# The output projection of a hybrid decoder layer: queueing the residual loads with their products, and a reversed order of token halves for the upper channels

## The chip, the cores and the metric

The kernel runs on one core of one Trainium2 chip. The metric is the device time of one execution in microseconds. In the trace PE is the matrix engine (its weight loads are listed as PEld), DVE the vector engine, ACT the scalar engine, POOL GpSimd, and SP the engine whose queue issues most of the loads.

## The reference

One layer of a hybrid decoder on 576 tokens (512 of a prompt and 64 of eight running sequences), width 1024. Two branches, an RWKV-7 scan and a differential attention, are merged by gates into `m`; then

```python
m = gate_a * (o_a @ lp['w_br_a']) + gate_b * (o_b @ lp['w_br_b'])
x = x + m @ lp['w_out']
hn = rmsnorm(x, lp['g_ffn'], NORM_EPS)
x = x + jnp.square(jax.nn.relu(hn @ lp['w_up'])) @ lp['w_down']
```

and a final RMSNorm. The change lies in the second of these lines and in how its result is made ready for `w_up`.

## The kernel before

Activations lie transposed, with channels on the 128 partitions and the 576 tokens along the free axis, so `x` is eight blocks of 128 channels (`d` = 0 to 7). Every fp32 product is made of three products of rounded halves: a tile is split into `hi` (ACT, a rounding copy) and `lo` (DVE, the rest), and PE adds hi·hi, hi·lo and lo·hi. The helper `dense` runs `stream`: the weights of one block of output channels are loaded by SP in two pieces of four 128x128 blocks (tiles `raw_...`, three buffers), each piece is split (`hi_...`, `lo_...`, three buffers each), and then the two halves of the tokens (`HALF`, 288 each) are computed one after the other, 24 matmuls each, into one of two PSUM banks (`ps_...`). When a half is done, `evac` is called for it.

The stage of the change is the loop of line 1085, over d = 0, 4, 1, 5, 2, 6, 3, 7. For each d it loads a block of x's rows (`xr`, two buffers, line 1087), and `evac` (here `ev`, line 1091) adds it to the product (`ya`, DVE), scales by g_ffn (`hf`, ACT) and puts the result, split in two, into blocks for the next stage. That stage, `up_pair`, multiplies by `w_up` by a scheme with seven products of quarter size in place of eight; so it wants not only the blocks b11 (channels 0 to 3, first half of tokens), b21 and b22 (channels 4 to 7, first and second half) but also the sums t1, t2, t3 and t4 of blocks. With lower block h of channel k and upper block h' of channel k + 4: t1 = second half of h minus first half of h; t2 = second half of h' minus t1; t3 = second half of h' minus second half of h; t4 = first half of h' minus t2. Each goes through `put`: an ACT copy and a DVE subtraction. `up_pair` uses them in the order t1, b11, t2, b21, t3, b22, t4. Behind each d, ACT squares the block and POOL adds it to `acc` for the norm.

The order on each engine's queue is made by a planner when the program is built: among the instructions whose predecessors and whose tile's place in memory are ready, it takes the one with the smallest priority number. By default that number is the place in the program, counted up from zero; `prio(at)` sets another. Loads of weights have `FEED + 1000 * job` with FEED = -1000000, where `job` counts the products in order, so every one of them is taken ahead of what has a default number. Evacuations have `FEED + 1000 * job + 200`. The loads of `w_up` (tiles `a`, line 1143) have the number of a job behind all eight of this stage. On the chip each queue keeps the order that it was given, and an instruction at its head that waits holds up all behind it. The load of `xr` has the default number. The places of `xr`, `hf` and `a` in memory were held before by tiles of the stage ahead of this one, the last of which are `g` (the gates that the branch product `ps_bra` is merged with), whose last reader is the DVE instruction that makes `ml`.

Of the kernel before, what the change touches and what calls it, by code (L numbers as in the profile page):

```python
# [8 lines left out]
F32 = mybir.dt.float32  # L9
# [6 lines left out]
P = 128  # L16
D = 1024
KT = D // P
# [10 lines left out]
HALF = ((0, 288), (288, 288))  # L29
# [12 lines left out]
def tile_hybrid_step(ctx, tc, xT, xsT, ktab, vtab, s0T, ptab, w_in, vecs, w2a2, g2, lamv,  # L42
                     w_bra, w_brb, w_out, w_up, w_down, cst, bias_p, bias_s,
                     yT, kTo, vTo, Sp, Ss, sh):
    nc = tc.nc
# [3 lines left out]
    def pool(name, bufs=1, stack=ctx, **kw):  # L49
        return stack.enter_context(tc.tile_pool(name=name, bufs=bufs, **kw))  # L50

    def f32(ap):
        return ap.bitcast(F32)

    ring = {"job": 0}

    def act(out, in_, func=AF.Copy, **kw):
        ring["act"] = AE.activation(out=out, in_=in_, func=func, **kw)  # L58

    def tt(out, a, b, op, eng=None):  # L60
        ins = (eng or VE).tensor_tensor(out=out, in0=a, in1=b, op=op)  # L61
        if eng is None:
            ring["tt"] = ins
# [19 lines left out]
    FEED, LATE, FILL = -1000000, 500000, 1000000  # L83

    @contextmanager
    def prio(at):
        was, tc.cur_priority = tc.cur_priority, at
        yield
        tc.cur_priority = was

    MUL, ADD, SUB, MAX = ALU.mult, ALU.add, ALU.subtract, ALU.max
# [42 lines left out]
    def v(i, n=1):  # L134
        return vec[:, i:i + n]
# [65 lines left out]
    def finish(gen, at=None):  # L201

        n = 0
        if at is None:
            at = next(gen, None)
        while at is not None:
            with prio(FILL + at + n):
                at = next(gen, None)
            n += 1

    def dense(*args, **kw):
        finish(stream(*args, **kw))
# [53 lines left out]
    with tc.tile_pool(name="xin", bufs=2, reuse_waits="tile") as xin:  # L266
# [6 lines left out]
        for k in range(0, KT, 4):  # L273
            for j in range(3):
                with prio(FEED + 1000 + 10 * k + j):
                    name = f"raw_{'qkv'[j]}0_{k}"
                    if k == 0:
                        raw = ring["pool"].tile([P, 4, P], F32, tag="raw", name=name, bufs=3)
                    else:
                        raw = zw.tile([P, 1 + NX], F32, tag="z" if j else "tz", name=name,  # L280
                                      bufs=2 if j else 1)[:, :4 * P].rearrange("p (k w) -> p k w", k=4)
# [152 lines left out]
    def gate(g):  # L434

        gg = gs.tile([P, NT], F32, tag="gg", name=f"gg{g}")

        def ev(ps, t0, n):
            tt(gg[:, t0:t0 + n], ps, R1[:, t0:t0 + n], MUL)
            act(gg[:, t0:t0 + n], gg[:, t0:t0 + n], AF.Tanh, scale=0.5)  # L440
        yield from stream(w_in[26 + g], KT, xh, xl, HALF, ev, f"g{g}")
        nc.sync.dma_start(out=gt_d[g], in_=gg)
# [20 lines left out]
    def branch_b(d):  # L463

        if not ob:
            ob.extend(ob_halves())
        gg = rt.tile([P, NT], F32, tag="T", name=f"gb{d}", bufs=6)
        nc.sync.dma_start(out=gg, in_=gt_d[KT + d])

        def ev(ps, t0, n):  # L470
            stt(gg[:, t0:t0 + n], gg[:, t0:t0 + n], 1.0, ps, ADD, MUL)
        yield from stream(w_brb[d], HB, ob[0], ob[1], HALF, ev, f"brb_{d}")
        nc.sync.dma_start(out=gt_d[KT + d], in_=gg)
# [160 lines left out]
    for h in range(HB):  # L634
        if h:
            qkv(h)
        for cc in range(2):
            GE.tensor_copy(
                out=qbd[64 * cc:64 * cc + 64, :, h, 8 * cc:8 * cc + 8],
                in_=qT[64 * cc:64 * cc + 64, h, NPR:].rearrange("p (b q) -> p b q", b=NB))  # L640
# [406 lines left out]
    mh = mp.tile([P, KT, NT], F32R, name="mh")  # L1047
    ml = mp.tile([P, KT, NT], F32R, name="ml")
    for d in range(KT):
        g = []  # L1050
        for i in range(2):
            gg = rt.tile([P, NT], F32, tag="T", name=f"g{i}_{d}", bufs=6)
            nc.sync.dma_start(out=gg, in_=gt_d[KT * i + d])
            g.append(gg)

        def ev(ps, t0, n, d=d, g=g):
            a, b = (x[:, t0:t0 + n] for x in g)
            stt(a, a, 1.0, ps, ADD, MUL)
            tt(a, a, b, ADD)
            act(mh[:, d, t0:t0 + n], a, scale=0.5)  # L1060
            stt(ml[:, d, t0:t0 + n], a, 0.5, f32(mh[:, d, t0:t0 + n]), MUL, SUB)
        dense(w_bra[d], HB, [o[:, 0] for o in oab], [o[:, 1] for o in oab], HALF, ev, f"bra_{d}")
# [15 lines left out]
    wt_ = pool("wt", 2, stack=fin, side="right", reuse_waits="tile")  # L1078

    def put(n, k, src):  # L1080
        act(hb[n][:, 0, k], src)
        tt(hb[n][:, 1, k], src, f32(hb[n][:, 0, k]), SUB)

    hfs = {}
    for i, d in enumerate((0, 4, 1, 5, 2, 6, 3, 7)):
        xr = wt_.tile([P, NT], F32, tag="xr", name=f"xr{d}")
        nc.sync.dma_start(out=xr, in_=xT[:, d])
        hf = hfs[d] = wt_.tile([P, NT], F32, tag="hf", name=f"hf{d}", bufs=3)
        k = d % 4

        def ev(ps, t0, n, d=d, k=k, xr=xr, hf=hf):
            x, h = ya[:, d, t0:t0 + n], hf[:, t0:t0 + n]
            tt(x, ps, xr[:, t0:t0 + n], ADD)
            act(h, x, scale=v(V_GF + d))
            if d < 4:
                if t0 == 0:
                    put("b11", k, h)
                else:
                    t1 = wt_.tile([P, 288], F32, tag="t", name=f"t1_{k}", bufs=4)
                    tt(t1, h, hf[:, :288], SUB)  # L1100
                    hfs["t1", k] = t1
                    put("t1", k, t1)
            elif t0 == 0:
                put("b21", k, h)
            else:
                t2 = wt_.tile([P, 288], F32, tag="t", name=f"t2_{k}", bufs=4)
                t3 = wt_.tile([P, 288], F32, tag="t", name=f"t3_{k}", bufs=4)
                t4 = wt_.tile([P, 288], F32, tag="t", name=f"t4_{k}", bufs=4)
                tt(t2, h, hfs["t1", k], SUB)
                put("t2", k, t2)  # L1110
                tt(t3, h, hfs[k][:, 288:], SUB)
                put("t3", k, t3)
                put("b22", k, h)
                tt(t4, hf[:, :288], t2, SUB)
                put("t4", k, t4)
        dense(w_out[d], KT, mh, ml, HALF, ev, f"wo{d}")
        sq = (M2, R2)[i % 2]
        act(sq, ya[:, d], AF.Square)
        if i == 0:
            GE.tensor_copy(out=acc, in_=sq)  # L1120
        else:
            tt(acc, acc, sq, ADD, GE)
# [137 lines left out]
    for d, n in enumerate((None, "t1", "b11", "t2", "b21", "t3", "b22", "t4")):  # L1260
        if n:
            t = fp.tile([P, 2, 4, 288], F32R, tag=f"h_{n}", name=f"w3_{d}", bufs=1)
            t = t.rearrange("p i k t -> p (i k t)")
# [179 lines left out]
```

## Time and profile before

| | |
|---|---|
| median of 3 runs | 1041.78 us (1041.49 to 1045.85) |
| the profiled execution, its own time | 1044.17 us |
| its span in the trace | 1042.4 us |
| PE busy | 1004.3 us, 96% of the span |
| the stage of the change | its first matmul starts at 578.7 us, its last at 639.6 us |

The profile is of one execution. A timeline row gives the start in us from the span's start, the busy time in us, the engine, the line, the operation with output and inputs, and in square brackets how long the engine was idle ahead of it and what it waited for. Rows that merge several instructions of a kind carry a count (x3). Matmuls overlap, so their pace is the distance from one start to the next, not the busy time of a row.

### The profile page before, as it was taken

Reading aid. Unit: us, or ns where it says so; the run is one execution under the profiler, and the core shown is the slowest. Engines: PE = TensorE matmul, PEld = TensorE weight load, DVE = VectorE, ACT = ScalarE, POOL = GpSimd, SP = SyncE. Lnnn points to the kernel's source line nnn. Section 1 sums busy time; section 2 is a strip of 40 time slices with the busy share of each in tenths; the row PEclk is TensorE's granted clock in tenths of the full one; section 3 lists DMA queues with packets and bytes.
Section 4 is the critical chain, followed back from the end, with each engine's and each line's share of the span. In section 5 each row is a group of like instructions: output and inputs, shape, how many; then the busy total and the mean of one; then the engine's idle time right before and its main releaser. Section 6 shows DMA issues by size and latency. Waiting matters only on the chain.

```text
span 1042.4 us, 24557 instructions
## 1 busy us (share of the span) xinstructions
PE 1004.3 (96%) x10088; PEld 931.2 (89%) x10088; DVE 690.2 (66%) x1445; ACT 498.5 (48%) x1090; POOL 94.9 (9%) x173
## 2 busy tenths in 40 slices
PE   9999989999999999999999799999999999999996
PEld 8989777888887879887889799999999999999996
DVE  6787545674856578435568788976666666666754
ACT  7575544443436344434334456655444444444732
POOL 1511100201010231000120021000000000000001
PEclk9999999999999989999999899999999999999998
DMA  7422444311112124322258542232222322221302
GB/s 273 170 81 76 135 147 139 94 45 51 36 53 65 45 94 146 98 67 89 90 172 253 187 123 86 82 102 82 91 89 86 100 91 82 91 82 41 112 21 91
DMA packets 50817, 105.75 MB, mean 101 GB/s; under 512 B 6050, under 2 KB 8098, under 8 KB 50578
## 3 DMA queue, kind: packets, MB, share of 16 engines
q1 hardware_dynamic: 47426, 96.95, 28.9%
q0 software_dynamic: 1648, 5.35, 1.4%
q8 instruction: 79, 1.29, 0.5%
q10 hardware_dynamic: 1632, 1.89, 0.5%
q14 instruction: 32, 0.26, 0.1%
HBM read 89.38 MB, written 14.78 MB: 100 GB/s over the span
## 4 chain that ended last, share of the span: by engine, by line
PE 77%; DVE 6%; ACT 5%; issue 5%; DMA 4%; POOL 2%; SPq 0%; DVEq 0%; POOLq 0%; ACTq 0%
PE ps_dn L72 20%; PE ps_g L72 10%; PE ps_z L72 7%; PE ua L1179 5%; PE ux L1179 5%; PE ps_bra L72 2%; PE uc L1179 2%; PE ps_k L72 2%; PE ud L1179 2%; PE ub L1179 2%; PE ps_q L72 2%; DMA kp<-in_ktab_dram 2%; PE pch L72 2%; PE pA L72 2%; PE pY L72 1%
## 5 line engine op out<-in xcount | busy, mean ns | idle before, releaser
L72 PE MATMUL ps_dn<-q,hi_dn 128*128 128x288 f32 x768 | 154.8, 296 | 0.0
L72 PEld LDWEIGHTS ps_dn<-q,hi_dn 128*128 128x128 f32 x768 | 122.8, 188 | 1.4
L72 PE MATMUL ps_dn<-q,lo_dn 128*128 128x288 f32 x384 | 113.2, 295 | 0.0
L72 PE MATMUL ps_g<-xh,lo_g 128*128 128x288 f32 x256 | 81.8, 319 | 0.1
L72 PE MATMUL ps_g<-xh,hi_g 128*128 128x288 f32 x256 | 81.1, 317 | 0.0
L72 PE MATMUL ps_g<-xl,hi_g 128*128 128x288 f32 x256 | 81.1, 317 | 0.0
L72 PEld LDWEIGHTS ps_dn<-q,lo_dn 128*128 128x128 f32 x384 | 72.0, 188 | 0.0
L72 PE MATMUL ps_z<-xh,hi_z 128*128 128x288 f32 (+1 forms) x224 | 69.1, 309 | 0.4 <-ACT hi_z L58 0.4
L72 PE MATMUL ps_z<-xh,lo_z 128*128 128x288 f32 (+1 forms) x224 | 69.5, 312 | 0.0
L72 PE MATMUL ps_z<-xl,hi_z 128*128 128x288 f32 (+1 forms) x224 | 68.7, 307 | 0.0
L61 DVE TENSOR_TENSOR ya<-ya,ps_dn 128x288 f32<-128x288 f32 x96 | 43.4, 452 | 29.4 <-PE ps_dn L72 29.3
L58 ACT ACTIVATE hi_dn<-raw_dn 128x512 fp32r<-128x512 f32 x48 | 30.1, 628 | 56.2 <-PE ps_dn L72 56.1
L1179 PE MATMUL ua<-h_b,hi 128*128 128x288 f32 x256 | 53.3, 298 | 0.4 <-ACT p L58 0.4
L72 PEld LDWEIGHTS ps_g<-xh,hi_g 128*128 128x128 f32 x256 | 50.2, 196 | 3.5 <-issue 1.6
L72 PEld LDWEIGHTS ps_g<-xh,lo_g 128*128 128x128 f32 x256 | 50.1, 196 | 3.0 <-issue 0.7
L72 PEld LDWEIGHTS ps_g<-xl,hi_g 128*128 128x128 f32 x256 | 50.0, 195 | 3.1 <-issue 0.8
L1179 PE MATMUL ux<-h_t,hi 128*128 128x288 f32 x256 | 52.3, 296 | 0.0
L58 ACT ACTIVATE c<-c 128x288 f32<-128x288 f32 x112 | 48.4, 439 | 6.5 <-DVE c L61 4.9
L58 ACT ACTIVATE hi<-a 128x1024 fp32r<-128x1024 f32 (+1 forms) x32 | 27.0, 845 | 42.7 <-PE ps_dn L72 34.8
L61 DVE TENSOR_TENSOR lo<-s,hi 128x1024 fp32r<-128x1024 f32 x32 | 39.7, 1239 | 10.5 <-ACT hi L58 10.4
L72 PE MATMUL ps_dn<-q,w 128*128 128x320 f32 (+1 forms) x336 | 46.3, 297 | 0.0
L72 PE MATMUL ps_wo<-mh,hi_wo 128*128 128x288 f32 x128 | 38.9, 304 | 7.6 <-DVE ya L61 7.6
(400 smaller groups left out, 2831.1 us busy)
## 6 DMA issues: line engine op xcount, KB each, us to landing
a<-in_w_up_dram SPq DMA_DIRECT2D x32, 512.0 KB, 3.3
raw_dn<-in_w_down_dram SPq DMA_DIRECT2D x64, 256.0 KB, 2.8
raw_g<-in_w_in_dram SPq DMA_DIRECT2D x32, 256.0 KB, 3.1
raw_z<-in_w_in_dram SPq DMA_DIRECT2D x28, 256.0 KB, 3.0
gt_d<-gg SPq DMA_DIRECT2D x16, 288.0 KB, 2.5
g<-gt_d SPq DMA_DIRECT2D x16, 288.0 KB, 4.0
kp<-in_ktab_dram SPq DMA_DIRECT2D x16, 256.0 KB, 3.9
vp<-in_vtab_dram SPq DMA_DIRECT2D x16, 256.0 KB, 3.9
```

What stands on the lines that cost most here:

```text
L58: ring["act"] = AE.activation(out=out, in_=in_, func=func, **kw)
L61: ins = (eng or VE).tensor_tensor(out=out, in0=a, in1=b, op=op)
L72: ring["mm"] = PE.matmul(out=out, lhsT=lhsT, rhs=rhs, start=start, stop=stop)
L1179: ring["mm"] = PE.matmul(out=ps[:, :288], lhsT=l[:, k], rhs=hb[blk][:, h, k], start=start and i == 0, stop=i == 11, skip_group_check=skip)
```

## The change

The load of `xr` gets the priority number one below the weight loads of its own product. For the upper channels (d of 4 and more) the two halves of the tokens are computed in the other order, the second first, and the sums are made as their inputs come: with the second half t2, t3 and b22, with the first half b21 and t4. Nothing is computed that was not before, and the same operations are issued in the same number.

```diff
     for i, d in enumerate((0, 4, 1, 5, 2, 6, 3, 7)):
         xr = wt_.tile([P, NT], F32, tag="xr", name=f"xr{d}")
-        nc.sync.dma_start(out=xr, in_=xT[:, d])
+        with prio(FEED + 1000 * (ring["job"] + 1) - 1):
+            nc.sync.dma_start(out=xr, in_=xT[:, d])
...
-            elif t0 == 0:
+            elif t0:
+                for n, x, y in (("t2", h, hfs["t1", k]), ("t3", h, hfs[k][:, 288:])):
+                    t = hfs[n] = wt_.tile([P, 288], F32, tag="t", name=f"{n}_{k}", bufs=4)
+                    tt(t, x, y, SUB)
+                    put(n, k, t)
+                put("b22", k, h)
+            else:
                 put("b21", k, h)
-            else:
-                t2 = wt_.tile([P, 288], F32, tag="t", name=f"t2_{k}", bufs=4)
-                t3 = wt_.tile([P, 288], F32, tag="t", name=f"t3_{k}", bufs=4)
                 t4 = wt_.tile([P, 288], F32, tag="t", name=f"t4_{k}", bufs=4)
-                tt(t2, h, hfs["t1", k], SUB)
-                put("t2", k, t2)
-                tt(t3, h, hfs[k][:, 288:], SUB)
-                put("t3", k, t3)
-                put("b22", k, h)
-                tt(t4, hf[:, :288], t2, SUB)
+                tt(t4, h, hfs["t2"], SUB)
                 put("t4", k, t4)
-        dense(w_out[d], KT, mh, ml, HALF, ev, f"wo{d}")
+        dense(w_out[d], KT, mh, ml, HALF[::1 if d < 4 else -1], ev, f"wo{d}")
```

## Rows read from the trace of the kernel before

**Rows 1.** The page: busy time, share of the span and instructions of each engine.

```profile
PE 1004.3 (96%) x10088; PEld 931.2 (89%) x10088; DVE 690.2 (66%) x1445; ACT 498.5 (48%) x1090; POOL 94.9 (9%) x173
```

**Rows 2.** Stretches of 5 us in and around the stage: from and to, length, busy time of each engine with its instructions, granted PE clock (1.00 is full), share and GB/s of the DMA engines.

```profile
585.00:590.00 5.00, 0.28 (x3) 0.04 (x1) 3.67 (x6) 2.16 (x3) 0.00 (x0) 0.86 0.86 285
590.00:595.00 5.00, 3.02 (x12) 3.02 (x13) 4.31 (x7) 3.73 (x7) 0.79 (x1) 0.50 0.45 137
595.00:600.00 5.00, 5.00 (x37) 5.00 (x37) 3.47 (x7) 1.24 (x3) 0.00 (x0) 0.95 0.29 97
600.00:605.00 5.00, 5.00 (x40) 5.00 (x39) 4.99 (x9) 2.94 (x8) 1.43 (x1) 1.00 0.54 156
605.00:610.00 5.00, 4.64 (x35) 4.44 (x34) 4.24 (x10) 3.72 (x8) 0.05 (x1) 1.00 0.29 71
```

**Rows 3.** Who waited for whom in the stage: engine and line, what it waited for, us in total, times, the longest.

```profile
PE ps_wo L72 <- DVE ya L61: 7.6, 3, 6.7
PE ub L1179 <- DVE h_t L61: 0.8, 1, 0.8
PE ua L1179 <- ACT p L58: 0.4, 1, 0.4
SPq L1143 <- DVE ml L66: 0.2, 1, 0.2
SPq L1087 <- DVE ya L61: 3.0, 4, 0.9
```

**Rows 4.** The chain of work that ended last, in order of time, across the wait: start, us, what.

```profile
587.00 4.45 DMA xr<-in_xT_dram
...
591.84 0.45 DVE ya L61
```

**Rows 5.** The timeline of SP's queue, merged, from 580 to 593 us.

```profile
580.67 1.77 SPq L1143 DMA_DIRECT2D a<-in_w_up_dram  x3
585.02 1.93 SPq L150 DMA_DIRECT2D raw_wo<-in_w_out_dram  x2
587.00 5.65 SPq L1087 DMA_DIRECT2D xr<-in_xT_dram  x3
```

**Rows 6.** Loads by tile, with the start of the issue and, in the line below, the us from issue to landing (least, median, most): the first `w_up` load, and all eight `xr`.

```profile
L1143 SPq DMA_DIRECT2D a<-in_w_up_dram x1: 607/607/607, 580.7 to 580.7; - x1
DMA to landing us min/median/max: 4.6/4.6/4.6
L1087 SPq DMA_DIRECT2D xr<-in_xT_dram x8: 328/350/425, 587.0 to 628.3; - x8
DMA to landing us min/median/max: 2.9/3.7/4.7
```

**Rows 7.** PE's timeline: the last matmul ahead of the wait, the first behind it (with the 13 between it and the third row at the slow pace), and the first two at full pace.

```profile
584.99 0.29 PE L72 MATMUL ps_wo<-mh,lo_wo 128*128 128x288 f32 x1
591.98 0.61 PE L72 MATMUL ps_wo<-mh,hi_wo 128*128 128x288 f32 x1 [6.70 <-DVE ya L61]
...
595.49 0.30 PE L72 MATMUL ps_wo<-mh,lo_wo 128*128 128x288 f32 x1
595.63 0.29 PE L72 MATMUL ps_wo<-mh,hi_wo 128*128 128x288 f32 x1
```

**Rows 8.** DVE's timeline in the wait (the preparation of the first pair of `w_up` blocks, from its first to its last instruction there) and right behind it.

```profile
586.54 0.69 DVE L61 TENSOR_TENSOR s<-a 128x512 f32<-128x512 f32 x1
...
589.55 1.23 DVE L61 TENSOR_TENSOR lo<-s,hi 128x1024 fp32r<-128x1024 f32 x1 [0.40 <-ACT hi L58]
591.47 0.82 DVE L61 TENSOR_TENSOR ya<-ps_wo,xr 128x288 f32<-128x288 f32 x2 [0.69 <-DMA xr<-in_xT_dram]
592.21 1.22 DVE L61 TENSOR_TENSOR lo<-a,hi 128x1024 fp32r<-128x1024 f32 x1
```

**Rows 9.** DVE behind the second half of d = 4, with the POOL instruction that runs meanwhile and the matmuls on both sides of PE's wait for the next evacuation, at the start of d = 5 and of d = 7.

```profile
601.43 0.45 DVE L61 TENSOR_TENSOR ya<-ps_wo,xr 128x288 f32<-128x288 f32 x1
603.23 1.68 DVE L61 TENSOR_TENSOR t<-hf,t 128x288 f32<-128x288 f32 x1
606.32 0.44 DVE L61 TENSOR_TENSOR ya<-ps_wo,xr 128x288 f32<-128x288 f32 x1
603.17 1.43 POOL L61 TENSOR_TENSOR acc<-acc,R 128x576 f32<-128x576 f32 x1 [8.49 <-ACT R L58]
606.25 0.29 PE L72 MATMUL ps_wo<-mh,lo_wo 128*128 128x288 f32 x1
606.90 0.37 PE L72 MATMUL ps_wo<-mh,hi_wo 128*128 128x288 f32 x1 [0.35 <-DVE ya L61]
632.42 0.29 PE L72 MATMUL ps_wo<-mh,lo_wo 128*128 128x288 f32 x1
633.25 0.37 PE L72 MATMUL ps_wo<-mh,hi_wo 128*128 128x288 f32 x1 [0.54 <-DVE ya L61]
```

**Rows 10.** The end of the stage: PE where the third of the seven products (`ub`, which reads t2) and the fourth (`ua`, which reads b21) wait.

```profile
644.09 0.29 PE L1179 MATMUL ub<-h_t,hi 128*128 128x288 f32 x1
645.19 0.40 PE L1179 MATMUL ub<-h_t,hi 128*128 128x288 f32 x1 [0.81 <-DVE h_t L61]
645.43 0.29 PE L1179 MATMUL ub<-h_t,lo 128*128 128x288 f32 x1
646.11 0.53 PE L1179 MATMUL ua<-h_b,hi 128*128 128x288 f32 x2 [0.39 <-ACT p L58]
```

## The prediction

> **What bounds the kernel now.** I read the page first: PE is busy 96% of the span [rows 1], so the kernel ends when PE's work ends, and only what makes PE wait, or run slowly, is worth removing. The stretches of 5 us find such a place at the start of the stage: between 585 and 595 us PE is busy 3.3 of 10 us, and the granted clock falls to 0.50 [rows 2], the lower of its two levels (1.2 GHz against 2.4). The list of waits gives the reason: of 7.6 us that PE waits for evacuations `ya`, one wait is 6.7 us [rows 3]. The chain in order of time says what is late: the load of `xr` for d = 0, issued at 587.00, takes 4.45 us, and then come its two evacuations [rows 4]. Both PSUM banks hold finished halves of d = 0 until then. Last I read SP's queue: three loads of `w_up` at 580.67, two pieces of `w_out` at 585.02 (each behind the release of its buffer), and only then `xr` [rows 5]. So the load was not slow; it was issued late, because its default priority put it behind everything with a number of FEED. Its memory was there: the first `w_up` load, whose pool opens at the same place of the program, left at 580.67, with only 0.2 us of waiting for the last readers of `g` [rows 3, 5].
>
> **The change, part by part.** Nothing is added or removed; loads and subtractions move.
>
> First, the load. With its new number it beats the `w_up` loads and the default ones, so I place the first `xr` where the first `w_up` load stood, 580.7, and the second `xr` behind it. It could stand earlier only if the planner opened the pool earlier, which would change nothing more. Landing: eight loads of this tile took 2.9 to 4.7 us [rows 6], so it lands at 583.6 to 585.4, and one evacuation (0.45 us [rows 4]) frees the bank at 584.1 to 585.9. PE wants it one matmul behind 584.99 [rows 7], at 585.12. Charge: 0 to 0.8 us; I take 0.3, nearer to the lower end, because the load now has only a `w_out` piece ahead of it, where the late one shared the DMA engines at 86% [rows 2].
>
> What that returns: from 584.99 to 591.98 is 6.99 us where 0.13 is the pace (595.49 to 595.63 is 0.14, with rounding) [rows 7]: 6.86 us. Then the clock: the 14 distances from 591.98 to 595.49 sum to 3.51 us [rows 7]; at full pace they are 14 x 0.134 = 1.87. That is 1.64 us more, gone if PE does not stand still. A wait of up to 0.8 us in its place is no reason to expect a fall: around the wait of 0.5 us at 606 the clock stayed at 1.00 [rows 2, 9].
>
> What is moved past: the two `xr` issues push three `w_up` loads and two `w_out` pieces later by two issues, under 1 us (three loads take 1.77 [rows 5]). The `w_out` pieces wait for their buffers until 585.02 anyway; the `w_up` tiles are wanted by PE some 50 us later. They cost nothing. For later d an `xr` waits at the head of SP's queue for the evacuation that frees its buffer; it did that before as well, 3.0 us in four waits [rows 3], and what stands behind it is a weight piece for the next product but one.
>
> Second, the work that had filled the wait. Between 586.54 and 591 us DVE, with PE standing still, prepared the first `w_up` pair, and at 592.21 it made one more `lo` [rows 8]. That is 590.78 - 586.54 = 4.2 us of work, plus 1.2, 5.4 in all, which must now fit between evacuations; DVE was already at 4.99 of 5 us from 600 to 605 [rows 2]. Lower bound 0, since an evacuation has the smaller number and two banks allow it 24 matmuls, 3.2 us; upper bound 5.4, if all of it stands in front of evacuations. The nearest row is the wait at 606: DVE crowded as much there, and PE lost 0.65 - 0.13 = 0.52 us [rows 9]. I charge two such, 1.0 us.
>
> Third, the order of the halves. Before, the second half of an upper channel brings eight DVE instructions at once (its addition, t2, t3, t4 and four `lo`). Behind the one at 601.43 the next evacuation came at 606.32 [rows 9], 4.9 us, more than the 3.2 us that a bank may wait. So PE lost 0.52 us there and 0.83 - 0.13 = 0.70 us at 632.42 [rows 9]: 1.2 us. Now six instructions come with the first product half and four with the second, in the same sum. I take half of the 1.2, 0.6, as gain (bounds 0 and 1.2).
>
> Fourth, the end of the stage. The third product of `up_pair` reads t2 and waited 0.8 us, the fourth 0.4 us [rows 3]; by distances PE lost 1.10 - 0.13 = 0.97 and 0.68 - 0.13 = 0.55 [rows 10], 1.5 us. With the second half first, t2 of d = 7 is made a half (3.2 us) sooner. What is last is then b21 and t4; b21 is first read by the fourth product, three products or 36 matmuls (4.8 us) behind the stage's last matmul, and its chain (addition 0.45, then `hf`, `put`; four instructions of about half a microsecond) takes some 2 us. The cover is those three products; without it the 2 us would show. I take 1.4 of 1.5 (bounds 0 and 1.5).
>
> **A rule weighed.** POOL's sum `acc` ran from 603.17 for 1.43 us, and DVE's t4, begun at 603.23, took 1.68 us [rows 9] where a like instruction takes 0.45: some 1.2 us lost. The Trainium skill, page "SBUF — State Buffer", section "Who interferes with whom", says that a DVE instruction with two SBUF inputs and a GpSimd one that reads SBUF take turns on a shared port, the second waiting until the first is through. The trace agrees with that (1.68 against 1.43 plus the rest). The rule speaks against the change, as b21 and t4 now come right when POOL runs: by it alone DVE would lose 1.43 us more behind each of four upper channels, were it not that t4 stood in that place before.
>
> **Sum.** 6.86 + 1.64 + 0.6 + 1.4 - 0.3 - 1.0 = 9.2 us. The profiled execution took 1044.17 us by its own time (span 1042.4), so its like would take 1035.0; it lies 2.4 us above the median, from which I forecast: 1041.78 - 9.2 = 1032.6.
>
> **The rivals.**
> A. As forecast, with its own range from 1030.6 (all of 6.86 + 1.64 + 1.2 + 1.5 = 11.2 gained) to 1034.5.
> B. DVE takes the place of the load. The 5.4 us of preparation and the POOL turns delay evacuations, and PE waits in pieces. For it speaks DVE at 4.99 of 5 us [rows 2]; against it the 3.2 us that a bank may wait. 11.2 - 0.8 - 5.4 = 5.0 us saved: 1036.8.
> C. The load does not move: the planner still puts `xr` behind the two `w_out` pieces. Then only the order of halves gains, 0.6 + 1.4 = 2.0: 1039.8. For it: I infer the pool's opening from one `w_up` load. Against it: that load left at 580.67 with a larger number than `xr` now has.
> D. Slower: an `xr` at the head of SP's queue waits for the evacuation two products back, and all `w_out` pieces of its product stand behind it. From the end of that product to halved weights it is then addition 0.45, issue 0.35, landing up to 4.7 [rows 6], and `hi` and `lo` together about 1.3, 6.8 us, where a product lasts 48 x 0.134 = 6.4. It decides when evacuations are late: to eat 9.2 us, six products must lose 1.5 us each, so each evacuation 1.1 us late. At 2 us late it is 6 x 2.4 = 14.4 lost, net +5.2: 1047. Against it: before, pieces left as soon as their buffers were free, well ahead of the `xr` of their product [rows 5].
>
> **How the numbers follow.** About 0.5% (5.2 us, so 1036.6) is what a measurement here can tell from no change. Chances: A 0.72, B 0.16, C 0.07, D 0.05. A and half of B, whose time lies at that bound, are faster: 0.72 + 0.08 = 0.80; the other half of B and C are the same: 0.15; D is slower: 0.05. The predicted time is A's. The range starts at A's best less half a microsecond for the spread of runs, 1030, and reaches to 1037.5, past B; left out are C, D and A's and B's tails, under 0.2.
>
> **What would show it.** Right: SP issues `xr` at or before 581, ahead of the `w_up` loads; the wait of 6.7 us is gone and the clock stays at 1.00 from 580 to 645; `ub` and the second `ua` begin without a wait; the last matmul of the stage starts near 631.8 (639.6 less 6.86 + 1.64 + 0.6 - 1.3). Wrong: PE waits of some 0.5 to 2 us for `ya` between 588 and 606 (B), an `xr` still at 587 (C), or PE waiting for `lo_wo` (D).

## The result, and the profile after

The changed kernel takes 1034.3 us (median of six runs, 1030.57 to 1036.83), the kernel before beside it 1042.83 us (six runs, 1040.38 to 1045.85). The ratio is 0.9912, with a 95% interval of 0.9884 to 0.9940: faster by 8.5 us between the medians, inside the range and 1.7 us above the forecast. The profiled execution took 1036.83 us by its own time, with a span of 1035.1 us.

Where did the time go? A stage is compared best by distances inside one trace, because what lies ahead of it shifts everything: here the stage begins 1.28 us later than before. First the matmuls of the stage (`ps_wo`) and of the first later product that the change doesn't touch (`ps_dn`, the first product with `w_down`), with the start of the first and the last at the end of each row. In the kernel before:

```profile
L72 PE MATMUL ps_wo<-mh,hi_wo x128: 289/295/606, 578.7 to 639.3; 128*128 128x288 f32 x128
...
L72 PE MATMUL ps_dn<-q,hi_dn x768: 288/295/400, 666.4 to 955.8; 128*128 128x288 f32 x192
```

and in the changed one:

```profile
L72 PE MATMUL ps_wo<-mh,hi_wo x128: 289/294/370, 580.0 to 632.7; 128*128 128x288 f32 x128
...
L72 PE MATMUL ps_dn<-q,hi_dn x768: 288/295/400, 659.2 to 948.7; 128*128 128x288 f32 x192
```

From the first `ps_wo` to the first `ps_dn` it was 87.7 us and is 79.2 (with the timeline's second decimal 87.63 and 79.23, 8.40 us less). The longest matmul of the stage, 606 ns before, is gone too: that was one at the low clock.

The queue of SP shows the step that this rests on, and answers [rows 5]:

```profile
575.16 6.70 SPq L150 DMA_DIRECT2D raw_wo<-in_w_out_dram  x3
581.95 0.90 SPq L1088 DMA_DIRECT2D xr<-in_xT_dram  x2
582.90 0.90 SPq L1142 DMA_DIRECT2D a<-in_w_up_dram  x2
587.09 0.33 SPq L1088 DMA_DIRECT2D xr<-in_xT_dram  x1
587.51 0.86 SPq L150 DMA_DIRECT2D raw_wo<-in_w_out_dram  x2
```

Two `xr` now stand where the `w_up` loads stood: 581.95 is 1.93 us behind the stage's first matmul (580.02), as 580.67 was before (578.74). DVE's first evacuations come at

```profile
585.52 0.46 DVE L61 TENSOR_TENSOR ya<-ps_wo,xr 128x288 f32<-128x288 f32 x1 [2.67 <-DMA xr<-in_xT_dram]
...
586.61 0.45 DVE L61 TENSOR_TENSOR ya<-ps_wo,xr 128x288 f32<-128x288 f32 x1
```

DVE is the one that waits for the load now. PE wants the first bank at 586.39, 0.4 us after the evacuation, and goes on at its pace of 0.13 us. The stretches of 5 us (columns as in [rows 2]):

```profile
585.00:590.00 5.00, 5.00 (x40) 5.00 (x39) 3.77 (x8) 3.46 (x7) 0.66 (x1) 1.00 0.94 319
590.00:595.00 5.00, 5.00 (x41) 5.00 (x40) 5.00 (x12) 4.23 (x8) 0.00 (x0) 1.00 0.61 203
595.00:600.00 5.00, 5.00 (x40) 5.00 (x39) 5.00 (x7) 3.25 (x8) 1.67 (x1) 1.00 0.49 156
600.00:605.00 5.00, 4.71 (x36) 4.48 (x35) 4.61 (x9) 3.91 (x8) 1.57 (x1) 1.00 0.48 129
605.00:610.00 5.00, 4.13 (x32) 3.90 (x31) 5.00 (x12) 3.70 (x9) 0.45 (x1) 1.00 0.52 162
```

PE is at 5.00 with the clock at 1.00 where it had been at 0.28 and 3.02 with the clock at 0.50 in the second. But DVE is full or nearly full from 590 on, and PE pays between 600 and 610. The list of waits says for what (engine, line, awaited, us in total, times, longest; PEld is the same wait seen by the weight load); it answers [rows 3]:

```profile
PEld ps_wo L72 <- DVE lo_wo L61: 2.0, 3, 1.1
PEld ua L1178 <- ACT p L58: 1.2, 1, 1.2
PE ps_wo L72 <- DVE lo_wo L61: 1.2, 2, 0.9
PE ua L1178 <- ACT p L58: 1.0, 1, 1.0
```

The list has no wait for `ya` any more, and none for t2 (`h_t`). In their place stand waits for the split weights `lo_wo`, and the wait for `p`, 0.4 before, has become 1.0. By distances between matmuls the `lo_wo` waits cost 0.45, 1.03 and 0.26 us, and 0.1 more each in the slow start behind them: 2.06 us. What is left at evacuations is 0.13 us.

### The profile page after: what moved, and what is told of

Its sections match the earlier page's. It is cut to its first block, busy times and chain, and to the rows that moved or that the text cites. A ratio compares the mean times of both kernels' runs of the same rounds, so it can differ in the third digit from the quotient of the medians.

```text
span 1035.1 us, 24556 instructions
## 1 busy us (share of the span) xinstructions
PE 1003.5 (97%) x10088; PEld 931.1 (90%) x10088; DVE 687.4 (66%) x1445; ACT 497.8 (48%) x1090; POOL 95.4 (9%) x173
## 4 chain that ended last, share of the span: by engine, by line
PE 75%; DVE 8%; DMA 5%; ACT 5%; issue 5%; POOL 2%; SPq 0%; DVEq 0%; POOLq 0%; ACTq 0%
PE ps_dn L72 20%; PE ps_g L72 10%; PE ps_z L72 6%; PE ua L1178 5%; PE ux L1178 5%; PE ps_k L72 3%; DMA kp<-in_ktab_dram 2%; PE uc L1178 2%; PE ud L1178 2%; PE ub L1178 2%; PE ps_q L72 2%; PE pch L72 2%; PE pA L72 2%; PE pY L72 1%; PE ps_v L72 1%
## 5 line engine op out<-in xcount | busy, mean ns | idle before, releaser
L72 PEld LDWEIGHTS ps_z<-xh,hi_z 128*128 128x128 f32 x224 | 43.4, 194 | 2.7 <-issue 1.4
```

The lines of the kernel that those rows point to most:

```text
L72: ring["mm"] = PE.matmul(out=out, lhsT=lhsT, rhs=rhs, start=start, stop=stop)
```

## The experiments

All distances are from the first `ps_wo` matmul, from the timelines: to the first matmul of `up_pair` (`uc`; it contains the stage) and to the first `ps_dn` (it contains the end of the stage as well). The kernel before took 1043.76 us (median of 11) beside the first four, 1040.06 (median of 14) beside the last four.

| kernel | to `uc`, us | to `ps_dn`, us | time, us | ratio to before |
|---|---|---|---|---|
| before | 60.95 | 87.63 | | |
| after | 53.07 | 79.23 | 1034.3 | 0.9912 (0.9884 to 0.9940) |
| e1_load_only | 53.70 | 80.36 | 1033.64 | 0.9917 (0.9886 to 0.9948) |
| e2_order_only | 61.67 | 87.81 | 1041.46 | 0.9997 (0.9966 to 1.0027) |
| e3_p_early | 53.34 | 79.49 | 1033.81 | 0.9920 (0.9886 to 0.9955) |
| e4_acc_dve | 51.19 | 76.49 | 1032.22 | 0.9903 (0.9871 to 0.9935) |
| e5_behind_wup | (another order) | 79.95 | 1034.81, one run | |
| e6_hold | 52.92 | 79.08 | 1032.73, one run | |
| e7_load_acc | 51.31 | 76.79 | 1031.46 | 0.9907 (0.9875 to 0.9939) |
| e8_best | 51.30 | 76.03 | 1029.93 | 0.9907 (0.9876 to 0.9939) |

The times of the faster kernels can't be told apart; what follows rests on the distances. Each is from one traced execution. How far such distances differ by themselves e3 shows: its edit acts behind `uc`, and yet it comes to `uc` 0.27 us later than the changed kernel, because its first `xr` landed later. Differences of two or three tenths are thus no finding.

**The load alone.** The kernel before with only the first part of the diff:

```diff
-        nc.sync.dma_start(out=xr, in_=xT[:, d])
+        with prio(FEED + 1000 * (ring["job"] + 1) - 1):
+            nc.sync.dma_start(out=xr, in_=xT[:, d])
```

> Only the priority of the xr load is changed; the order of the token halves is that of before. Theory (late load): nearly the whole gain is here. From the first matmul of ps_wo to the first of ps_dn the kernel before takes 87.6 us and the changed one 79.2; this one 80.4 (6.86 + 1.64 - 0.3 - 1.0 less), about 7 us faster than before in time. The waits at the first uses of t2 and of p at the end of the stage stay (1.5 us), and those for late evacuations at d = 5 and d = 7 too. Rival (the two edits need each other: with DVE's work no longer spread over the wait, the eight instructions of the old second half delay evacuations by 2 to 3 us more): 82.5 to 83.5, about 4.5 us faster.

Measured: 80.36 us to `ps_dn`, 7.27 less than before, of the changed kernel's 8.40. The waits of the old order are all there still:

```profile
PE ps_wo L72 <- DVE ya L61: 0.8, 2, 0.5
PE ub L1180 <- DVE h_t L61: 0.8, 1, 0.8
PE ps_wo L72 <- DVE lo_wo L61: 0.4, 1, 0.4
PE ua L1180 <- ACT p L58: 0.4, 1, 0.4
```

The load is nearly all of the change: 7.25 of the 7.88 us that are won up to `uc` come with it alone. What PE still lost up to `uc`, by distances and with the slow starts, is 0.55 us for the first evacuation, 1.28 at later evacuations and 0.94 for `lo_wo`. The 0.55 are no part of the order: d = 0 is computed alike in both kernels. `xr` was issued at 578.38, 1.93 us behind the stage's first matmul as in the changed kernel, but the first evacuation began 4.38 us later, against 3.57 there. The issue of this load took 0.87 us, where it took 0.42 in the changed kernel; why is open.

**The order alone.** The changed kernel with the load at its default number:

```diff
-        with prio(FEED + 1000 * (ring["job"] + 1) - 1):
-            nc.sync.dma_start(out=xr, in_=xT[:, d])
+        nc.sync.dma_start(out=xr, in_=xT[:, d])
```

> Only the order of the halves and of the sums is changed; the xr load has its default priority. Theory (late load): the wait of 6.7 us and the low clock stay; 86.0 us from the first ps_wo to the first ps_dn (0.6 to 1.1 from the evacuations at d = 5 and 7, and 0.5 at the end), 1.5 us faster than before, not to be told from it in time. Rival (the order is what matters): 80 us, 7 us faster.

Measured: 87.81 us, 0.18 more than before, and no difference in time. A miss of 1.8 us. PE's timeline and the stretches show where it went: into a wait that lies ahead of the first half the order touches, and into the slow matmuls behind it.

```profile
589.95 0.61 PE L72 MATMUL ps_wo<-mh,hi_wo 128*128 128x288 f32 x1 [6.91 <-DVE ya L61]
590.35 0.44 PE L72 MATMUL ps_wo<-ml,hi_wo 128*128 128x288 f32 x1
...
595.63 0.44 PE L72 MATMUL ps_wo<-mh,lo_wo 128*128 128x288 f32 x1
```

```profile
590.00:595.00 5.00, 5.00 (x21) 5.00 (x22) 4.10 (x6) 2.24 (x5) 0.79 (x1) 0.50 0.57 162
595.00:600.00 5.00, 5.00 (x36) 5.00 (x36) 4.41 (x10) 2.75 (x6) 0.00 (x0) 0.90 0.00 2
```

The wait was 7.21 us by distances, 0.22 more than before, and 25 distances behind it are slow, against 14 before: 11 x (0.24 - 0.134) = 1.17 us. That the order has no part in these 1.39 us is argued from their place, not shown. Without them it is worth 1.21 us beside a late load: 0.67 ahead of `uc` and 0.54 behind it. Beside an early load it is worth less: from e1 to the changed kernel the distance falls by 80.36 - 79.23 = 1.13, of which 0.55 are e1's late landing. Of the other 0.58, 0.63 - 0.55 = 0.08 lie ahead of `uc` and 0.50 behind it. Ahead of `uc` the order took 1.28 - 0.13 = 1.15 us from the waits for evacuations and added 2.06 - 0.94 = 1.12 to those for `lo_wo`.

**Why the end of the stage gave so little: memory for `p`?** The wait for `p` had grown. First theory: `p` is late because its memory, held before by this stage's tiles, opens late. So p went into a tile that is free earlier:

```diff
-            p1 = e("p1")
+            p1 = e("p1") if f1 else M2[:, :288]
```

> The changed kernel, with the copy p of the first pair written to M2, a tile of a pool that is open already, in place of a tile whose pool opens when the last tile of the w_out stage is given back. Theory (p is issued late, since the planner may place it only behind the last put): the wait of 1.1 us in front of the second ua goes; 78.1 us from the first ps_wo to the first ps_dn (changed kernel 79.2), too little to be seen in time. Rival (the fourth product waits for b21, or ACT is simply full): the wait stays at 1 us with another name, 79.2.

Measured: 79.49 us, and the wait stayed:

```profile
PE ps_wo L72 <- DVE lo_wo L61: 1.2, 2, 0.9
PE ua L1178 <- ACT M L58: 0.9, 1, 0.9
```

The theory fell: the memory isn't what `p` waits for. (`M` is `p` in its new place.)

**POOL's sums.** In the changed kernel's trace, instructions of DVE with two inputs in SBUF stretch where POOL adds a square to `acc`: six of 128x288 take 1.09 to 1.69 us, where others of the kind take 0.45, and each ends 0.32 us behind POOL's. One of them, and POOL's sum beside it:

```profile
596.80 1.69 DVE L61 TENSOR_TENSOR h_b<-hf,h_b 128x288 fp32r<-128x288 f32 x1
```

```profile
596.50 1.67 POOL L61 TENSOR_TENSOR acc<-acc,R 128x576 f32<-128x576 f32 x1 [7.30 <-ACT R L58]
```

DVE ended at 598.49, a third of a microsecond behind POOL's 598.17: it did most of its own work when POOL was through. The kernel before has seven such instructions, so this price is not new. The experiment gives the sums to DVE:

```diff
-            tt(acc, acc, sq, ADD, GE)
+            tt(acc, acc, sq, ADD)
```

> The changed kernel, with the seven sums of squares made by DVE in place of POOL. Theory (the remaining waits for lo_wo at 601, 608 and 628 us, 2.0 us, come from DVE instructions held up while POOL runs, 1.2 us each): a sum costs DVE 0.7 to 0.8 us in place of 1.2, so 1 to 1.5 of the 2.0 us go; 52.0 us from the first ps_wo to the first uc (changed kernel 53.1). Rival (it is the amount of DVE's work between 585 and 610 us): DVE gets 0.75 us more for each block, the waits stay or grow; 53.1 to 54.5.

Measured: 51.19 us to `uc`, 1.88 less than the changed kernel, and 76.49 to `ps_dn`, 2.74 less: a larger gain than the theory's 52.0 to `uc`, and against the rival. Of the `lo_wo` waits one of 0.13 us by distance is left, 0.23 with its slow start, and no instruction of that kind takes as much as 0.8 us. On DVE:

```profile
631.89 0.76 DVE L61 TENSOR_TENSOR acc<-acc,R 128x576 f32<-128x576 f32 x1
632.57 0.45 DVE L61 TENSOR_TENSOR h_b<-hf,h_b 128x288 fp32r<-128x288 f32 x1
```

DVE got more work and yet came out ahead: a sum costs it 0.76 us, where POOL's cost `h_b` 1.69 - 0.45 = 1.24. This is the rule of the Trainium skill that the prediction weighed (page "SBUF — State Buffer", section "Who interferes with whom"); the run agrees with it: with POOL's seven sums the stretched instructions went, and all but 0.23 of the 2.06 us of waits for `lo_wo`.

**How early must the load be?** The number of `xr` was set one above that of the first `w_up` loads, to see what one or two large loads ahead of it cost:

```diff
-        with prio(FEED + 1000 * (ring["job"] + 1) - 1):
+        with prio(FEED + 1000 * (ring["job"] + 9 - i) + 1):
```

> The changed kernel, with the xr loads numbered right behind the w_up loads of the first pair: the first xr stands behind two loads of 512 KB in SP's queue. Theory (it is the place in the queue, and what shares the DMA engines, that sets when xr lands): issued about 0.9 us later and landing 4.4 to 5.8 us on, as the w_up loads did, so PE waits 1.5 to 3 us for the first evacuation, and 81 to 82.5 us pass from the first ps_wo to the first ps_dn (changed kernel 79.2). Rival (only being ahead of the two w_out pieces counts): no wait above 0.6 us, 79.2.

Measured: 79.95 us, between the two. The planner put one `w_up` load ahead, not two:

```profile
579.29 0.38 SPq L1142 DMA_DIRECT2D a<-in_w_up_dram  x1
579.73 0.42 SPq L1088 DMA_DIRECT2D xr<-in_xT_dram  x1
580.25 0.37 SPq L1142 DMA_DIRECT2D a<-in_w_up_dram  x1
```

```profile
584.09 0.82 DVE L61 TENSOR_TENSOR ya<-ps_wo,xr 128x288 f32<-128x288 f32 x2 [0.48 <-DMA xr<-in_xT_dram]
```

Issued at 579.73, the load let the first evacuation begin 4.36 us later. PE lost 1.00 - 0.13 = 0.87 us there, and the clock didn't fall. It fits neither the theory (a wait of 1.5 to 3 us) nor the rival (none above 0.6). Counted from the end of its own issue, the load took 3.94 us to its first evacuation here, and 3.0 to 3.5 in the seven traces where it stands first in the queue. So a `w_up` load ahead cost its issue of 0.4 us and perhaps half a microsecond of landing, by one execution; two ahead weren't seen. Later waits for `ya` (0.22, 0.24 and 0.86) go with another order of what follows, in which PE began `up_pair` early.

**The place of `p` on ACT's queue.** ACT's timeline in the changed kernel, at the end of the stage:

```profile
637.11 0.43 ACT L58 ACTIVATE h_t<-t 128x288 fp32r<-128x288 f32 x1
638.02 0.63 ACT L58 ACTIVATE hi<-a 128x512 fp32r<-128x512 f32 x1 [0.47 <-DMA a<-in_w_up_dram]
638.55 0.39 ACT L58 ACTIVATE p<-ua 128x288 f32<-128x288 f32 x1
```

The product that `p` copies had its last matmul at 636.15, ahead of the third product. But on ACT's queue `p` stands behind the split (`hi<-a`) of a `w_up` block that only the third call of `up_pair` wants, two calls later, and that split waits for its load. Second theory: this order costs the wait. The split is put behind `p`:

```diff
-        A22 = halve(a22, False, 7)
+        with tc.issue_after(ring["p", 0]) if f1 == 4 else ExitStack():
+            A22 = halve(a22, False, 7)
...
             act(p1, ba[:, :288])
+            ring["p", f1] = ring["act"].ins
```

> The changed kernel, with ACT's split of the second half of the third pair's w_up block queued behind the copy p of the first pair, and nothing else moved. Theory (p stands on ACT's queue behind that split, which waits for a w_up load to land): the wait of 1.1 us in front of the second ua goes down to 0.2 or less; 78.2 us from the first ps_wo to the first ps_dn. Rival (the fourth product waits for b21 anyway): a wait of about 1 us stays, 79.2.

Measured: the wait for `p` is gone, so the place was right. To `ps_dn` it is 79.08 us, only 0.15 less, and these 0.15 lie ahead of `uc`; from `uc` to `ps_dn` it is 26.16 us in both kernels. The list of PE's waits has a new row:

```profile
PE ux L1179 <- DVE c L61: 1.1, 1, 1.1
PE ps_wo L72 <- DVE lo_wo L61: 0.9, 1, 0.9
```

The seventh product adds to the bank `ux` after DVE has read the fifth's result from it. DVE, with splits of `w_up` blocks ahead, reads it only at 639.98, and PE stands from 639.04 to 640.49.

```profile
638.48 1.22 DVE L61 TENSOR_TENSOR lo<-a,hi 128x1024 fp32r<-128x1024 f32 x1
639.61 0.45 DVE L61 TENSOR_TENSOR q<-c,q 128x288 fp32r<-128x288 f32 x1
639.98 0.45 DVE L61 TENSOR_TENSOR c<-ux,w 128x288 f32<-128x288 f32 x1
```

A stall was moved from ACT's queue to DVE's.

**Is the order still worth something with DVE relieved?** The load and the sums on DVE, with the old order:

```diff
 # the kernel before, with e1's load, and
-            tt(acc, acc, sq, ADD, GE)
+            tt(acc, acc, sq, ADD)
```

> The old order of halves, the new priority of xr, and the sums of squares on DVE. Theory (the old order's eight instructions crowd one half whatever POOL does, and t2 comes last): the waits for late evacuations at d = 5 and 7 shrink to 0 to 0.5 us each, that for t2 shrinks too, since t4 isn't held up in front of it, but stays at 0.5 us or more; 77.5 to 78.5 us from the first ps_wo to the first ps_dn, 1 to 2 us more than with both edits and the sums on DVE (76.5). Rival (once DVE is relieved the order is worth nothing): 76.5.

Measured: 76.79 us against 76.49 with the new order: 0.3 us, about what two executions differ by, where it was 0.58 beside an early load and 1.21 beside a late one. The theory (77.5 to 78.5) fell. With DVE relieved, either order lets evacuations come nearly in time, up to `uc` (51.31 and 51.19), and the wait for t2 is gone with the old order too.

**Both remedies together.** The changed kernel with the edits of e4 and of e6.

> The changed kernel with the sums of squares on DVE and the split of the third pair queued behind the copy p. Theory (the two add): 76.5 less 0.5 is 76.0 us from the first ps_wo to the first ps_dn, about 3 us faster than the changed kernel and 11.6 us faster than before. Rival (moving the split behind p makes its own reader late): 76.5 to 77.

Measured: 76.03 us, 3.2 less than the changed kernel; PE's list of waits is empty in the stage. Its time, 1029.93 us, has a ratio to before whose interval overlaps the changed kernel's, so that it is the fastest is shown by the distances alone. e6's edit is worth 0.46 us on top of e4 (0.57 won behind `uc`, 0.11 lost ahead of it), where alone it won nothing behind `uc`: with DVE relieved, the stall at `ux` doesn't take its place.

## Why the prediction was right, and where its sum was off

**The cause and its size: right.** The load was late in its queue and not slow. At the place that was forecast the wait of 6.86 us and the 1.64 us of low clock went, and clock and PE stood as foretold. e1 bears out that part by itself: 6.86 + 1.64 - 0.3 - 1.0 = 7.2 was forecast for the load up to `uc`, 7.25 was measured. The last matmul of the stage was to start near 631.8 on the time axis of before. It started at 633.0, which is 631.7 less the shift of 1.28 us.

**Up to `uc`: the sum right, three of its terms not.** 6.86 + 1.64 + 0.6 - 0.3 - 1.0 = 7.8 was forecast, 7.88 measured. By distances the landing cost nothing (0.3 charged; 0.55 in e1, both inside its bounds). The waits at evacuations fell from 1.50 us with their slow starts to 0.13, a gain of 1.37 where half of 1.2, 0.6, was taken. And DVE's crowding cost 2.06 where 1.0 was charged. The errors of +0.3, +0.8 and -1.1 cancel: luck, where e1's agreement isn't quite (there the landing and `lo_wo` cost 0.55 and 0.94, near the charges). The two larger errors belong together: from e1 to the changed kernel the order took 1.15 us from the waits for evacuations and put 1.12 on those for `lo_wo`. So up to `uc` it was worth 0.08 us beside the early load, and not the 0.6 of the sum; of the 0.63 us between the two kernels 0.55 are a later landing in e1.

**DVE's crowding came at another place.** The prediction looked at evacuations, which have the smaller number and kept their time. What came late were the split weights `lo_wo`, waits that it had put down as the sign of rival D. It wasn't D: DVE was busy all through 605 to 610, and e4 removed nearly all of these waits without a change to SP's queue. It was B's mechanism at two fifths of B's price (2.06 of 5.4), and POOL's turns, which the prediction had named, were what made it dear: all but 0.23 of the 2.06 us went with them.

**The end of the stage (1.4 taken of 1.5): 0.5, the step that was mis-sized.** The wait for t2, 0.97 us, went as forecast. The wait for `p` was counted with it, though its row in the list [rows 3] named an ACT copy and not t2. What stood ahead of that copy in the kernel before are the copy of t4 and the split; t4 itself, and behind it the `lo` of t2 that the third product waited for, were late beside POOL's sum of 643.01:

```profile
643.07 1.69 DVE L61 TENSOR_TENSOR t<-hf,t 128x288 f32<-128x288 f32 x1
644.69 0.45 DVE L61 TENSOR_TENSOR h_t<-t,h_t 128x288 fp32r<-128x288 f32 x1
...
644.80 0.44 ACT L58 ACTIVATE h_t<-t 128x288 fp32r<-128x288 f32 x1 [0.86 <-DVE t L61]
645.15 0.61 ACT L58 ACTIVATE hi<-a 128x512 fp32r<-128x512 f32 x1
645.67 0.39 ACT L58 ACTIVATE p<-ua 128x288 f32<-128x288 f32 x1
```

There the copy of t4 held `p` up, and the split did not wait: its load, issued at 641.4, had landed 3.1 us later, at 644.5. The new order removed this hold. But the load stood right behind it. It lands 4.8 us after the first `uc` matmul in both kernels, about when PE, no longer stopped by t2, comes to the fourth product (36 matmuls, 4.8 us). So in the changed kernel the split waits for its load, e6 shows that this is the cause of the wait there, and the wait grew from 0.55 to 1.12 us. So 0.97 - 0.57 = 0.4 was left, near the 0.50 by distances. The prediction's cover for b21 (three products) held: PE waited for nothing of b21.

**The sum.** Forecast up to `ps_dn`: 9.2; measured 8.40 there, and 8.64 to the end of the last matmul. In the two profiled executions the spans differ by 7.3 us, which is 8.64 less the 1.28 that the stage began later. The 0.8 us missing are the end of the stage, 1.4 - 0.5 = 0.9. Of the 1.7 us by which the time lies above the forecast, the other part, 1.05 us, is that the kernel before measured 1042.83 us beside it and not 1041.78.

**The rivals.** C is refuted by SP's queue. D: no piece of `w_out` came late by an `xr` ahead of it that PE's waits show. B was there, and smaller than priced. Of the signs of being right one failed: the second `ua` began behind a wait.

## What to carry to other kernels

When a row of waits names a copy on another engine, read all that stands ahead of that copy in its queue, and when each of it could have begun, before the wait is counted as part of an edit's gain: here one hold went, and the next, a prefetch's split that waits for its load, took its place. A load that is late by its place in a queue is worth its wait and the slow matmuls behind it, and the trace of before shows its new place: the issue of a neighbour whose memory opens at the same point. And an engine that looks free may be a bad place for small work: moving seven sums from POOL to the full DVE shortened the stage and its end by 2.7 us.

## What the runs showed of the hardware

Two things were not expected. The slow matmuls behind a long wait differ in number for nearly the same wait: 14 distances of 0.23 to 0.40 us behind 6.99 us in the kernel before, 25 behind 7.21 us in e2, some 1.2 us apart. In these two executions a stage with such a wait differs by about as much as a small edit brings. And waits of 1.0 and 1.3 us (1.16 us between two starts in the changed kernel at 607.76, 1.44 in e6 at 639.04, with 0.13 as the pace) left the granted clock at 1.00.
